# State-space tables computed during the dense projections, kept in DRAM and loaded back; the output stage by token block

## The chip, the cores and the metric

The kernel runs on one core of one Trainium2 chip. The metric is the device time of one execution in microseconds (us). The engines are TensorE (PE: matmuls, with PEld for its weight loads), VectorE (DVE), ScalarE (ACT), GpSimd (POOL) and SyncE (SP, which issues transfers). DMA transfers are issued from SP, ACT and POOL.

## What is computed

One inference step of one decoder layer for a prompt of 1024 tokens and 8 samples of 4 tokens, all in f32 (each large product as three products of a high and a low part):

```python
xn = rms_norm(x, ln1_g); proj = xn @ w_in             # 1024 -> u | q | k | v, 512 each
# S5 group, 32 groups of 64 complex states, 16 channels each
dt = exp(ssm_log_dt); lb = exp(a * dt)                # complex a, lb
bb = ((lb - 1) / a)[..., None] * b
h_t = lb * h_{t-1} + bb @ u_t                         # the scan over tokens
y = Re(c @ h) + d * u;  g = gelu(y)
ssm_out = g * sigmoid(g @ ssm_glu_w)
# differential attention, 4 heads (two softmax maps, ALiBi); samples read paged keys and values
o = rms_norm(attend(q, k, v, lam), subln_g) * (1 - lam0)
x = x + concat(ssm_out, o) @ w_out
x = x + cross_attention(x, 256 memory tokens) @ ca_wo
x = x + (silu(conv3(xn @ ffn_wg)) * (xn @ ffn_wv)) @ ffn_wd
```

The prompt's scan is not run token by token: tokens go in chunks of 8, and tables made of powers of `lb` with `b` and `c` turn each chunk into matmuls. They depend on parameters alone.

## The kernel before

**Stages.** Tokens lie in columns (1056 of them, in blocks TB of 384, 384 and 288; the last block ends with the 32 sample columns). Up to the output projection the work is a set of Python generators that `drive` (L1483) interleaves by weight; the order in which they yield sets the priority of the instructions, and a scheduler then fixes one order for each engine's queue. The streams are: `dense_all` (heads 0 and 1, `dense_u` for the state-space input, heads 2 and 3; on the chip it ends at about 334 us), `params` (parameters of the state space, `ssm_params`), `attention_all` (four heads one after the other), `ssm_tables`, `ssm_datas` and `ssm_outs` (four sets q of 8 groups), `memory_kv` (keys and values of the memory), `samples` (paged attention of the samples) and `sample_state`.

**Tables.** `ssm_setup(q)` (L932) makes the tables of set q: `CLr`, `CLi` (six products of 128x576 on POOL), M in the space of `T` (six of 128x512, on POOL except for q = 3, on DVE), a 128x128 block `Kt` by 16 matmuls `kp` (L963) that goes to DRAM (`k_d`), `ST` by eight transposes `sp` (L976), and `Rr`, `Ri` (six products on POOL). Then POOL clears `T` (L989), and eight transfers on SP write shifted copies of `k_d` into it (L991). `ssm_tables` (L1077) starts after the dense projections ("right" marks the room that they leave), set 1 after attention of head 2, set 2 after the attention ("left") and set 3 after `ssm_data(0)`. The tables use three rooms `sqs[q % 3]` and two `sqs[q % 2]`. `ssm_data(q)` (matmuls `wp`, products and scans on DVE, giving `Hr`, `Hi`) and `ssm_out(q)` (matmuls `yp` with `T` and `CL`, gelu, transposes into `gT[q]`) use them.

**Attention.** `turn(t)` transposes probabilities into `aT`, which has `AB = 2` buffers (L776), and `value(t)` multiplies them with v after every second t.

**Output stage** (from L1493). x comes back from DRAM (`xT_d`) into `Xh`, `Xl` by four transfers on POOL, issued ahead of everything else of the stage (L1498); their room is partly that of the samples' tiles. `gate(d, b, ks)` multiplies `gT` with the glu weights for output block d and token block b, d in the outer loop. After the gates `turn_samples(1, ...)` turns the last sample heads, POOL writes them into the last columns of `mixT` (L1595), and `load_part` (L1528) loads each head's part of `mixT` for the three blocks and splits it over the place where `gT` was split. Then, for each of eight output blocks d, `load_cols` loads 128 columns of `w_out`, and `update_x` adds the product to x.

Of the kernel before, what the change touches and what calls it, by code (L numbers as in the profile page):

```python
# [20 lines left out]
SEQ = 1024  # L21
# [48 lines left out]
def hymba_step(ctx: ExitStack, tc: tile.TileContext, A: dict, O: dict, upto=99, dbg=None):  # L70
# [54 lines left out]
    k_d = dram.tile([512, 128], F32, name="k_d")  # L125
# [121 lines left out]
    nCi = sg.tile([128, 16, 16], F32, name="nCi")  # L247

# [201 lines left out]
    a2 = pool(p2, "a2", 1)  # L450
    hdB = pool(p2, "hdB", 1)
# [33 lines left out]
    st = Carve([hdB.tile([128, SEQ], F32, tag=t, name="scr") for t in ("qT", "kT", "vt", "s3", "s4")])  # L485
# [290 lines left out]
    AB = 2  # L776
# [92 lines left out]
    def params():  # L869
        yield from ssm_params(st, ps_t)  # L870
        done.add('params')

# [5 lines left out]
    gp = gT = sk = sd = ptb = sa = mk_ = zs = ps_w = ps_y = ps_x = Bbr = Bbi = M16 = fin = None  # L878
# [5 lines left out]
    def blk(pl, src, name, tag=None):  # L884
        b = pl.tile([128, 16, 2, 16], F32, name=name, tag=tag or name)
# [3 lines left out]
        return b  # L889

    def open_right():
        nonlocal sk, ptb, sa, mk_, Bbr, Bbi, M16, fin
        sk = pool(pk, "sk", 1, side="right")
        Bbr, Bbi = blk(sk, Br, "Bbr"), blk(sk, Bi, "Bbi")
        M16 = sk.tile([128, 16], F32, name="M16")
        nc.vector.tensor_reduce(out=M16, in_=ident.rearrange("p (g c) -> p c g", c=16), axis=AX.X, op=ALU.add)
# [32 lines left out]
    RE = 'GGGGGGGGGGVG'  # L929
    eng = {'G': nc.gpsimd, 'V': nc.vector}  # L930

    def ssm_setup(q):  # L932
        P4 = slice(4 * q, 4 * q + 4)
        sq_, st_ = sqs[q % 3], sqs[q % 2]
        tg = 'ta' if q > 1 else 'td'
        e, e2, e3 = (eng[c] for c in RE[3 * q:3 * q + 3])
        q1 = sk.tile([128, 4, 9, 16], F32, tag="q1", name="q1")
        q2 = sk.tile([128, 4, 9, 16], F32, tag="q2", name="q2")
        CLr = sq_.tile([128, 4, 9, 16], F32, tag="CLr", name="CLr")
        CLi = sq_.tile([128, 4, 9, 16], F32, tag="CLi", name="CLi")  # L940
# [13 lines left out]
        T = sq_.tile([128, 8, 128], F32, tag="T", name="T")  # L954
        Mr, Mi = (T[:, 4 * i:4 * i + 4].rearrange("p r (j c) -> p r j c", c=16) for i in range(2))
        cmul(e2, Mr, Mi, Rv[:, 0, P4].unsqueeze(3).to_broadcast(sh), Rv[:, 1, P4].unsqueeze(3).to_broadcast(sh),
# [3 lines left out]
        kp = tp("kp", tg)  # L960
# [5 lines left out]
        Kt = st_.tile([128, 128], F32, tag="Kt", name="Kt")  # L966
        nc.vector.scalar_tensor_tensor(out=Kt[:, 0:16], in0=M16, scalar=GT[:, 120 + q:121 + q], in1=kp[:, 0:16],
                                       op0=ALU.mult, op1=ALU.add)
        nc.scalar.copy(Kt[:, 16:], kp[:, 16:128])
        nc.scalar.dma_start(out=k_d[128 * q:128 * q + 128, :], in_=Kt)  # L970
        yield Z[2]
        ST = []
        for M in (Mr, Mi):
            sp = tp("sp", tg)
            for r in range(4):
                nc.tensor.transpose(sp[:, 128 * r:128 * r + 128], M[:, r].rearrange("p a b -> p (a b)"), ident)  # L976
            s = st_.tile([128, 4, 128], F32, tag=f"ST{len(ST)}", name="ST")
            nc.scalar.copy(fl(s), sp)
            ST.append(s)
            yield 440  # L980
        Rr = st_.tile([128, 4, 128], F32, tag="Rr", name="Rr")
        Ri = st_.tile([128, 4, 128], F32, tag="Ri", name="Ri")
        sh = [128, 4, 8, 16]
# [118 lines left out]
    def ssm_outs():  # L1102
        for q in range(4):
            yield from until(lambda: q in half)
            yield from ssm_out(q)
# [1013 lines left out]
```

## Time and profile before

| | us |
|---|---|
| median of 3 runs (lowest to highest) | 1847.84 (1842.98 to 1848.39) |
| the profiled execution | 1845.88 |
| its span, first to last instruction | 1844.1 |

The rest of the profiled execution's time, 1.8 us, lies around the span. An engine's busy time is not a cost by itself: where one engine is always busy, only its work counts; where none is, the waits between them do. The granted clock is the share of full speed that TensorE was given in a stretch; its two levels are 1.2 and 2.4 GHz.

### The profile page before, as it was taken

How to read it: one execution, taken by the hardware profiler on the slowest of the kernel's cores; microseconds unless marked ns; L12 is line 12 of the kernel's file. 1: busy time of each engine (PE TensorE's matmuls, PEld its weight loads, DVE VectorE, ACT ScalarE, POOL GpSimd, SP SyncE). 2: the span in 40 equal slices, each digit the busy share in tenths (PEclk: the TensorE clock that was granted, in tenths of full speed). 3: DMA queues.
4: the chain of work that ended last, by engine and by line, in shares of the span. 5: the costliest groups of instructions: out<-in, count | busy, mean ns of one | idle time of the engine just before them, and what ended most of it. 6: DMA issues, size and time to landing. Idle time of an engine off the chain costs nothing.

```text
span 1844.1 us, 28603 instructions
## 1 busy us (share of the span) xinstructions
PE 1717.8 (93%) x11121; PEld 1597.5 (87%) x11121; DVE 1105.2 (60%) x2569; ACT 604.1 (33%) x1368; POOL 487.8 (26%) x543
## 2 busy tenths in 40 slices
PE   8798999779787789999989999999999999999998
PEld 7587897558575689999868999999999999999998
DVE  7866446774896465655546664665555654655653
ACT  6554355545354243444533211111111111111112
POOL 4412411470710034100022332312322222223200
PEclk9898999789797989999989999999999999999999
DMA  5601212143365631233363021211101101201102
GB/s 172 233 26 59 64 48 60 59 127 121 117 204 179 239 90 51 87 98 98 98 196 107 24 61 35 58 32 50 58 24 58 58 24 58 58 24 59 55 15 96
DMA packets 151744, 155.76 MB, mean 84 GB/s; under 512 B 12535, under 2 KB 128915, under 8 KB 151610
## 3 DMA queue, kind: packets, MB, share of 16 engines
q1 hardware_dynamic: 131954, 106.57, 19.5%
q0 software_dynamic: 9152, 27.49, 4.6%
q10 hardware_dynamic: 10504, 19.88, 2.9%
q8 instruction: 87, 1.43, 0.3%
q14 instruction: 47, 0.39, 0.1%
HBM read 124.39 MB, written 29.51 MB: 83 GB/s over the span
## 4 chain that ended last, share of the span: by engine, by line
PE 78%; DVE 10%; DMA 4%; ACT 3%; issue 2%; POOL 0%; ACTq 0%; SPq 0%; DVEq 0%; POOLq 0%
PE pp L184 5%; PE pp L185 5%; PE pp L186 5%; PE pd L186 5%; PE pd L185 4%; PE pd L184 4%; PE pv L186 4%; PE pv L184 4%; PE pv L185 4%; PE pg L184 4%; PE pg L185 4%; PE pg L186 4%; PE pj L184 2%; PE pj L186 2%; PE pj L185 2%
## 5 line engine op out<-in xcount | busy, mean ns | idle before, releaser
L56 DVE TENSOR_TENSOR xacc<-xacc,pd 128x384 f32<-128x384 f32 (+1 forms) x264 | 135.1, 518 | 170.1 <-PE pd L186 170.1
L56 ACT CAST whi<-raw 128x1024 fp32r<-128x1024 f32 x74 | 77.6, 1050 | 435.6 <-PE pg L185 331.6
L186 PE MATMUL pv<-Xh,wlo 128*128 128x384 f32 (+1 forms) x528 | 171.8, 326 | 0.3 <-DVE wlo L56 0.3
L184 PE MATMUL pv<-Xh,whi 128*128 128x384 f32 (+1 forms) x528 | 172.1, 326 | 0.0
L185 PE MATMUL pv<-Xl,whi 128*128 128x384 f32 (+1 forms) x528 | 171.8, 325 | 0.0
L184 PE MATMUL pg<-Xh,whi 128*128 128x384 f32 (+1 forms) x528 | 171.3, 324 | 0.4 <-DVE hg L56 0.4
L184 PE MATMUL pd<-ah,dhi 128*128 128x384 f32 (+1 forms) x528 | 171.2, 325 | 0.1
L186 PE MATMUL pd<-ah,dlo 128*128 128x384 f32 (+1 forms) x528 | 170.9, 324 | 0.0
L185 PE MATMUL pd<-al,dhi 128*128 128x384 f32 (+1 forms) x528 | 170.1, 322 | 0.5 <-DVE al L56 0.5
L185 PE MATMUL pg<-Xl,whi 128*128 128x384 f32 (+1 forms) x528 | 170.6, 323 | 0.0
L186 PE MATMUL pg<-Xh,wlo 128*128 128x384 f32 (+1 forms) x528 | 170.1, 322 | 0.0
L184 PE MATMUL pp<-Mh,whi 128*128 128x384 f32 (+1 forms) x336 | 108.6, 332 | 18.5 <-ACT Mh L56 18.5
L56 DVE TENSOR_TENSOR wlo<-raw,whi 128x1024 fp32r<-128x1024 f32 x74 | 107.1, 1450 | 25.3 <-ACT whi L56 21.9
L793 POOL TENSOR_TENSOR raw<-raw,GT 128x1024 f32<-128x1024 f32 x30 | 70.6, 2354 | 163.4 <-DMA raw<-in_ffn_wg_dram 112.9
L185 PE MATMUL pp<-Ml,whi 128*128 128x384 f32 (+1 forms) x336 | 110.1, 330 | 0.2 <-DVE Ml L56 0.2
L186 PE MATMUL pp<-Mh,wlo 128*128 128x384 f32 (+1 forms) x336 | 110.0, 329 | 0.0
L184 PE MATMUL pj<-whi,Xh 128*128 128x384 f32 (+1 forms) x288 | 101.3, 353 | 5.6 <-DVE vt L56 4.0
L186 PEld LDWEIGHTS pv<-Xh,wlo 128*128 128x128 f32 x528 | 100.1, 190 | 0.5 <-DVE wlo L56 0.4
L186 PE MATMUL pj<-whi,Xl 128*128 128x384 f32 (+1 forms) x288 | 100.4, 349 | 0.0
L184 PEld LDWEIGHTS pv<-Xh,whi 128*128 128x128 f32 x528 | 100.1, 190 | 0.0
L185 PEld LDWEIGHTS pv<-Xl,whi 128*128 128x128 f32 x528 | 100.0, 189 | 0.0
L185 PEld LDWEIGHTS pd<-al,dhi 128*128 128x128 f32 x528 | 99.2, 188 | 0.8 <-DVE al L56 0.8
(792 smaller groups left out, 4514.5 us busy)
## 6 DMA issues: line engine op xcount, KB each, us to landing
raw<-in_ffn_wg_dram SPq DMA_DIRECT2D x22, 512.0 KB, 3.8
raw<-in_ffn_wv_dram SPq DMA_DIRECT2D x22, 512.0 KB, 3.8
raw<-in_ffn_wd_dram SPq DMA_DIRECT2D x22, 512.0 KB, 3.8
pg<-in_cache_k_dram SPq DMA_DIRECT2D x32, 256.0 KB, 2.7
V<-in_cache_v_dram SPq DMA_DIRECT2D x32, 256.0 KB, 5.2
kt<-in_cache_mem_k_dram SPq DMA_DIRECT2D x32, 256.0 KB, 2.8
vt<-in_cache_mem_v_dram POOLq DMA_DIRECT2D x16, 512.0 KB, 5.5
raw<-in_w_in_dram SPq DMA_DIRECT2D x48, 128.0 KB, 3.1
```

The source lines that it names most:

```text
L56: return f(*a, **k)
L184: nc.tensor.matmul(out, lhsT=wh, rhs=xh, start=start, stop=False)
L185: nc.tensor.matmul(out, lhsT=wh, rhs=xl, start=False, stop=False)
L186: nc.tensor.matmul(out, lhsT=wl, rhs=xh, start=False, stop=stop)
L793: nc.gpsimd.tensor_tensor(out=raw, in0=raw, in1=g.unsqueeze(2).to_broadcast([128, KD, 128]), op=ALU.mult)
```

## The change

- `params` goes on after the parameters with all four `ssm_setup(q)`, so that they run beside the dense projections. All their products are on POOL. They work in a pool `tb` of their own, and each set is written to DRAM: `cl_d` and `rr_d` from POOL, `st_d` and `k_d` from ACT. `Kt` is 240 columns wide, with 112 columns of zeros ahead, so that `T` needs no clearing.
- `ssm_load(q)`, called where `ssm_setup(q)` was, brings set q back by eleven transfers on POOL's queue. The conditions of sets 2 and 3 are new.
- `Bbr`, `Bbi` and `M16` are made early and live in a permanent pool. To make room the attention buffer `aT` is single (`AB = 1`) and one scratch tile is gone.
- In the output stage the gates run by token block, the sample heads are turned after block 1, the parts of block b are loaded after its gates, and x is loaded for each output block d on SP, ahead of that block's weights.

```diff
@@ tables
-    k_d = dram.tile([512, 128], F32, name="k_d")
+    k_d = dram.tile([512, 240], F32, name="k_d")
+    cl_d = dram.tile([4, 128, 1152], F32, name="cl_d")
+    st_d = dram.tile([4, 128, 1024], F32, name="st_d")
+    rr_d = dram.tile([4, 128, 1024], F32, name="rr_d")
...
+    tb = pool(p2, "tb", 1)
...
-    AB = 2
+    AB = 1
...
     def params():
         yield from ssm_params(st, ps_t)
+        blk(Bbr, Br)
+        blk(Bbi, Bi)
+        nc.vector.tensor_reduce(out=M16, in_=ident.rearrange("p (g c) -> p c g", c=16), axis=AX.X, op=ALU.add)
         done.add('params')
+        for q in range(4):
+            yield from ssm_setup(q)
...
     def ssm_setup(q):
-        tg = 'ta' if q > 1 else 'td'
-        e, e2, e3 = (eng[c] for c in RE[3 * q:3 * q + 3])
+        e = nc.gpsimd
+        CL = tb.tile([128, 2, 4, 9, 16], F32, tag="CL", name="CLt")
...
+        nc.gpsimd.dma_start(out=cl_d[q], in_=CL.rearrange("p i r j c -> p (i r j c)"))
...
-        kp = tp("kp", tg)
+        kp = tp("kp", "td")
...
-        Kt = st_.tile([128, 128], F32, tag="Kt", name="Kt")
+        Kt = tb.tile([128, 240], F32, tag="Kt", name="Kt")
+        nc.gpsimd.memset(Kt[:, 0:112], 0.0)
...
+        nc.scalar.dma_start(out=st_d[q], in_=ST.rearrange("p i n -> p (i n)"))
...
-        nc.gpsimd.memset(T, 0.0)
+        nc.gpsimd.dma_start(out=rr_d[q], in_=R_.rearrange("p i r n -> p (i r n)"))
+        yield 10
+
+    def ssm_load(q):
+        sq_, st_ = sqs[q % 3], sqs[q % 2]
+        ST = st_.tile([128, 2, 4, 128], F32, tag="ST", name="ST")
+        R_ = st_.tile([128, 2, 4, 128], F32, tag="R", name="Rr")
+        CL = sq_.tile([128, 2, 4, 9, 16], F32, tag="CL", name="CL")
+        T = sq_.tile([128, 8, 128], F32, tag="T", name="T")
+        nc.gpsimd.dma_start(out=ST.rearrange("p i r n -> p (i r n)"), in_=st_d[q])
+        nc.gpsimd.dma_start(out=R_.rearrange("p i r n -> p (i r n)"), in_=rr_d[q])
         for j in range(8):
-            nc.sync.dma_start(out=T[16 * j:16 * j + 16, :, 16 * j:],
-                              in_=k_d[128 * q:128 * q + 128, :128 - 16 * j].rearrange("(g c) f -> c g f", c=16))
+            nc.gpsimd.dma_start(out=T[16 * j:16 * j + 16],
+                                in_=k_d[128 * q:128 * q + 128, 112 - 16 * j:240 - 16 * j]
+                                .rearrange("(g c) f -> c g f", c=16))
+        nc.gpsimd.dma_start(out=CL.rearrange("p i r j c -> p (i r j c)"), in_=cl_d[q])
...
     def ssm_tables():
         yield from until(lambda: 'right' in done)
-        yield from ssm_setup(0)
+        ssm_load(0)
         yield from until(lambda: 2 in done)
         phA.close()
         sqs.append(pool(pk, "sqB", 1, side="right"))
-        yield from ssm_setup(1)
-        yield from until(lambda: 'left' in done)
-        yield from ssm_setup(2)
-        yield from until(lambda: ('data', D3) in done)
-        yield from ssm_setup(3)
+        ssm_load(1)
+        yield from until(lambda: 'left' in done and ('data', 0) in done)
+        ssm_load(2)
+        yield from until(lambda: ('data', 1) in done and ('out', 0) in done)
+        ssm_load(3)
@@ output stage
-    for k in range(0, KD, 4):
-        for i, X in enumerate((Xh, Xl)):
-            nc.gpsimd.dma_start(out=r32(X[:, k:k + 4]),
-                                in_=xT_d[i][128 * k:128 * k + 512, :].rearrange("(k p) n -> p k n", p=128))
...
-        for d in range(4):
-            for b in range(3):
+        for b in range(3):
+            for d in range(4):
                 if (d, b) not in early:
                     gate(d, b, (0, 1, 2, 3))
-        turn_samples(1, tail['os'], ps.tile([128, 512], F32, tag="pj", name="po"))
-        nc.gpsimd.dma_start(out=mixT[:, SEQ:].rearrange("(h p) t -> p h t", p=128), in_=qsT)
-        for h in range(NH):
-            load_part(wx, Mh, Ml, mixT, 128 * h, 4 + h)
+            if b == 1:
+                turn_samples(1, tail['os'], ps.tile([128, 512], F32, tag="pj", name="po"))
+                nc.gpsimd.dma_start(out=mixT[:, SEQ:].rearrange("(h p) t -> p h t", p=128), in_=qsT)
+            for h in range(NH):
+                load_part(wx, Mh, Ml, mixT, 128 * h, 4 + h, b)
         for d in range(KD):
+            for i, X in enumerate((Xh, Xl)):
+                nc.sync.dma_start(out=r32(X[:, d]), in_=xT_d[i][128 * d:128 * d + 128, :])
             hi, lo = load_cols(A['w_out'][0], d)
```

## Rows read from the trace of the kernel before

**Rows 1.** the page: the span, and the busy time of each engine.

```profile
span 1844.1 us, 28603 instructions
PE 1717.8 (93%) x11121; PEld 1597.5 (87%) x11121; DVE 1105.2 (60%) x2569; ACT 604.1 (33%) x1368; POOL 487.8 (26%) x543
```

**Rows 2.** busy PE, PEld, DVE, ACT, POOL by stretch; PEclk, DMA, GB/s.

```profile
95.00:334.00 239.00, 230.96 (x1322) 197.48 (x1321) 130.04 (x441) 118.35 (x389) 54.48 (x78) 0.97 0.17 49
334.00:446.00 112.00, 85.76 (x649) 67.89 (x647) 81.29 (x224) 59.19 (x150) 56.71 (x55) 0.82 0.37 111
...
466.00:560.00 94.00, 78.79 (x742) 64.60 (x742) 81.24 (x149) 38.27 (x69) 41.35 (x36) 0.85 0.57 173
560.00:590.00 30.00, 18.13 (x158) 12.46 (x154) 28.18 (x74) 17.05 (x31) 0.00 (x0) 0.72 0.43 125
...
620.60:634.50 13.90, 13.90 (x86) 13.62 (x84) 4.68 (x9) 3.02 (x6) 3.49 (x5) 1.00 0.97 347
634.50:650.60 16.10, 0.03 (x1) 0.00 (x0) 0.01 (x1) 0.43 (x1) 0.00 (x0) 0.60 0.83 316
650.60:660.00 9.40, 9.39 (x46) 9.39 (x47) 6.06 (x12) 4.28 (x9) 0.00 (x0) 0.77 0.49 141
```

**Rows 3.** the chain of waits, 466 to 650 us: start, us, what.

```profile
623.33 24.58 DMA mixT<-qsT
```

**Rows 4.** timeline of POOL: start, us, instruction [idle before it, releaser].

```profile
620.34 0.79 POOL L1498 DMA_DIRECT2D Xh<-xT_h  x1 [84.69 <-DMA ms<-mixT]
...
623.33 0.76 POOL L1595 DMA_DIRECT2D mixT<-qsT  x1
```

**Rows 5.** what PE waited for, 334 to 620 us: total, times, longest.

```profile
PE yp L1052 <- DVE Hr L56: 11.2, 3, 7.4
...
PE sp L976 <- ACT Kt L56: 4.3, 1, 4.3
```

**Rows 6.** groups on DVE, 334 to 600 us: xcount, busy us, mean ns.

```profile
L56 DVE TENSOR_TENSOR mwl<-mraw,mwh 128x1024 fp32r<-128x1024 f32 x16 | 23.2, 1454 | 17.2 <-ACT mwh L56 17.1
L56 DVE TENSOR_TENSOR_SCAN vr<-rho,vr 128x128 f32<-128x128 f32 x16 | 9.4, 643 | 0.0
...
L56 DVE TENSOR_TENSOR vr<-va,vb 128x512 f32<-128x512 f32 x4 | 7.1, 1775 | 0.0
L56 DVE TENSOR_TENSOR_SCAN vi<-rho,vi 128x128 f32<-128x128 f32 x16 | 6.7, 478 | 0.0
...
L56 DVE TENSOR_SCALAR yk<-vk 128x2 int32<-128x2 int32 x4 | 4.7, 1172 | 0.1
```

**Rows 7.** timeline of DVE at moments when POOL computes nothing.

```profile
446.53 0.17 DVE L56 TENSOR_SCALAR yk<-vk 128x2 int32<-128x2 int32 x1
...
514.93 0.68 DVE L56 TENSOR_TENSOR q<-Rv,Bi 128x512 f32<-128x512 f32 x1
...
538.50 0.67 DVE L56 TENSOR_TENSOR vr<-va,vb 128x512 f32<-128x512 f32 x1
...
540.41 1.36 DVE L56 TENSOR_TENSOR_SCAN vr<-rho,vr 128x128 f32<-128x128 f32 x4
...
542.27 1.22 DVE L56 TENSOR_TENSOR mwl<-mraw,mwh 128x1024 fp32r<-128x1024 f32 x1
```

**Rows 8.** PE and PEld busy, L963 (kp), then L976 (sp), 334 to 620.6 us.

```profile
334.00:620.60 286.60, 3.70 (x64) 2.18 (x64) 0.84 0.45 136
334.00:620.60 286.60, 6.37 (x32) 4.40 (x32) 0.84 0.45 136
```

**Rows 9.** groups on POOL, 334 to 560 us, the costliest.

```profile
L951 POOL TENSOR_TENSOR CLi<-q,q 128x576 f32<-128x576 f32 x4 | 6.5, 1631 | 0.3
```

**Rows 10.** timeline of PE in attention of head 3.

```profile
423.05 1.56 PE L727 MATMUL ov<-aT,vt 128*128 128x256 f32 x6
...
425.54 0.60 PE L719 MATMUL pt<-ident,P 128*128 128x128 f32 x4
```

**Rows 11.** transfers: issuer, xcount, KB each, median us to landing.

```profile
Ug<-u_p SPq DMA_DIRECT2D x4, 512.0 KB, 4.4
```

More of the change, by code (lines that the diff above doesn't have):

```diff
@@ L247, in hymba_step @@
     nCi = sg.tile([128, 16, 16], F32, name="nCi")
+    Bbr, Bbi = (sg.tile([128, 16, 2, 16], F32, name=n) for n in ("Bbr", "Bbi"))
+    M16 = sg.tile([128, 16], F32, name="M16")
     px = ctx.enter_context(ExitStack())
@@ L484, in hymba_step @@
     xt_ = [load_x(0)]
-    st = Carve([hdB.tile([128, SEQ], F32, tag=t, name="scr") for t in ("qT", "kT", "vt", "s3", "s4")])
+    st = Carve([hdB.tile([128, SEQ], F32, tag=t, name="scr") for t in ("qT", "kT", "vt", "s3")])
     grow = st.tile([128, 128], F32, name="grow")
@@ L882, in tp, with blk @@
         return ps_t.tile([128, 512], F32, tag=tag, name=name)
-    def blk(pl, src, name, tag=None):
-        b = pl.tile([128, 16, 2, 16], F32, name=name, tag=tag or name)
+    def blk(b, src):
         nc.gpsimd.memset(b, 0.0)
@@ L888, in blk @@
         nc.scalar.copy(b[64:128, :, 1, :], src[64:128])
-        return b
     def open_right():
-        nonlocal sk, ptb, sa, mk_, Bbr, Bbi, M16, fin
+        nonlocal sk, ptb, sa, mk_, fin
         sk = pool(pk, "sk", 1, side="right")
-        Bbr, Bbi = blk(sk, Br, "Bbr"), blk(sk, Bi, "Bbi")
-        M16 = sk.tile([128, 16], F32, name="M16")
-        nc.vector.tensor_reduce(out=M16, in_=ident.rearrange("p (g c) -> p c g", c=16), axis=AX.X, op=ALU.add)
         fin = sk.tile([128, 2, 16], F32, name="fin")
@@ L951, in ssm_setup @@
         e.tensor_tensor(out=CLi, in0=q1, in1=q2, op=ALU.subtract)
+        nc.gpsimd.dma_start(out=cl_d[q], in_=CL.rearrange("p i r j c -> p (i r j c)"))
         yield Z[0]
         sh = [128, 4, 8, 16]
[L954 to L956 removed]
+        M = tb.tile([128, 2, 4, 128], F32, tag="M", name="M")
+        cmul(e, M[:, 0].rearrange("p r (j c) -> p r j c", c=16), M[:, 1].rearrange("p r (j c) -> p r j c", c=16),
+             Rv[:, 0, P4].unsqueeze(3).to_broadcast(sh), Rv[:, 1, P4].unsqueeze(3).to_broadcast(sh),
              Br[:, P4].unsqueeze(2).to_broadcast(sh), Bi[:, P4].unsqueeze(2).to_broadcast(sh),
@@ L970, in ssm_setup @@
         nc.scalar.dma_start(out=k_d[128 * q:128 * q + 128, :], in_=Kt)
         yield Z[2]
-        ST = []
-        for M in (Mr, Mi):
-            sp = tp("sp", tg)
+        ST = tb.tile([128, 2, 512], F32, tag="ST", name="STt")
+        for i in range(2):
+            sp = tp("sp", "td")
             for r in range(4):
[L976 to L979, printed above, removed]
+                nc.tensor.transpose(sp[:, 128 * r:128 * r + 128], M[:, i, r], ident)
+            nc.scalar.copy(ST[:, i], sp)
@@ L1105, in ssm_outs @@
             yield from ssm_out(q)
+            done.add(('out', q))
     def ssm_sample(s):
@@ L1138, in ssm_sample @@
         hs = bus
-        Cbr, Cbi = blk(s, Cr, "Cbr", "uz"), blk(s, nCi, "Cbi", "bT")
+        Cbr, Cbi = (s.tile([128, 16, 2, 16], F32, name="Cb", tag=t) for t in ("uz", "bT"))
+        blk(Cbr, Cr)
+        blk(Cbi, nCi)
         st1 = s.tile([128, 16, 8], F32, name="st1")
@@ L1526, in token_rstd, with load_part @@
         rsqrt(pl, r, v, 9)
-    def load_part(pl, Mh, Ml, src, row, k):
-        for t0, n in TB:
-            ms = pl.tile([128, 384], F32, tag="xn", name="ms", bufs=4)
-            nc.sync.dma_start(out=ms[:, :n], in_=src[row:row + 128, t0:t0 + n])
-            split(Mh[k][:, t0:t0 + n], Ml[k][:, t0:t0 + n], ms[:, :n])
+    def load_part(pl, Mh, Ml, src, row, k, b):
+        t0, n = TB[b]
+        ms = pl.tile([128, 384], F32, tag="xn", name="ms", bufs=4)
+        nc.sync.dma_start(out=ms[:, :n], in_=src[row:row + 128, t0:t0 + n])
+        split(Mh[k][:, t0:t0 + n], Ml[k][:, t0:t0 + n], ms[:, :n])
     def load_cols_k(w, d):
```

25 lines of the change are left out of this document (9 added, 16 removed).

## The prediction, made before the changed kernel was run

> **What bounds the kernel now.** I read the busy shares first: TensorE (PE) is busy 93% of 1844.1 us [rows 1]. So a change pays only where PE idles or runs at the lower clock, and the next view is the table of stretches [rows 2]. It shows three kinds of stage. In the dense projections, 95 to 334 us, PE is busy 231.0 of 239.0 us: PE is the bound, 8.0 us are idle, and GpSimd (POOL) works only 54.5 us. From 334 to 590 us the last attention head, the memory keys, the samples and the state space run together, and no engine is full for long: PE is busy 85.8 of 112.0, then 78.8 of 94.0, then 18.1 of 30.0 us, at granted clocks of 0.82, 0.85 and 0.72. VectorE (DVE) is the busiest one there from 466 us on, with 81.2 of 94.0 and 28.2 of 30.0 us; these two stretches are near DVE's bound. In the third kind, at the output projection, PE does nothing for 16.1 us (634.5 to 650.6) and then starts at a granted clock of 0.77.
>
> The chain of waits says whose that last hole is: a single write, the 32 sample columns of the heads (mixT<-qsT), takes 24.58 us to land [rows 3]. POOL's timeline shows why: it was issued at 623.33, right behind the loads of x (4 issues of 2112 KB, from 620.34) on the same queue [rows 4]. The loads of the head parts, in order on SP, wait for that write from the third one on, and PE, at 0.03 us of matmuls in 16.10 us, waits for those [rows 2].
>
> **Part 1, the output stage.** Three edits act together. The gates run block by block, so the part loads of blocks 0 and 1 no longer stand behind the sample columns. The sample write no longer has the x loads ahead of it. And x comes in 16 loads of 528 KB on SP, behind the parts. PE then has matmuls of blocks 0 and 1 for output blocks d = 0, 1, ... while the sample columns travel; six accumulators of 24 matmuls at 0.16 us (86 in the 13.90 us before the hole [rows 2]) cover about 23 us. The hole goes: 16.1 us. So does the restart: 9.4 us at 0.77 of the clock means 4.3 us at the lower of the two levels, which cost half of that, 2.2 us [rows 2]. Sum: 18.3 us saved. The lower bound is 8: the sample output may now be wanted by PE earlier than it is ready, since only the gates of the last block stand between, or the first weights may queue on SP behind an x load that waits for its room until the samples end (before, at 620.34 [rows 4]). The upper bound is 20.
>
> By the Trainium skill, page "DMA: Bandwidth & Descriptors", section "Issuing engines are not separate DMA queues", transfers issued by different engines run on the same 16 DMA engines, and another issuer saves only issue time. By that, moving x from POOL to SP is worth nothing in itself, and what counts is that x is asked for after the parts and in small pieces. If it still overtook them, this part would be worth nothing, which is rival 4.
>
> **Part 2, the tables leave the stage from 334 to 590 us.** Each of four sets is 18 POOL products in this stage, except that one product set of q = 3 ran on DVE; a product lasts about 1.3 to 1.6 us (the longest group 1631 ns) [rows 9], and POOL is busy 56.7 and 41.4 us here [rows 2], most of it this. POOL itself is off the path. Its price is seen on DVE: the four scans take 1.36 us, one 128x512 addition 0.67 us, one weight remainder (mwl) 1.22 us and one tiny yk 0.17 us while POOL computes nothing [rows 7], but their means over the stage are 643 and 478 ns a scan, 1775, 1454 and 1172 ns [rows 6]. The excess of these five groups: 16 x (0.643 - 0.340) = 4.8, 16 x (0.478 - 0.340) = 2.2, 4 x (1.775 - 0.67) = 4.4, 16 x (1.454 - 1.22) = 3.7 and 4 x (1.172 - 0.17) = 4.0, together 19.1 us. To it come six products of q = 3 on DVE at 0.68, 4.1 us [rows 7], and one direct wait of PE for a table (sp<-Kt), 4.3 us [rows 5]. Total 27.5 us. How much is on the path? In 466 to 590 DVE is full enough that I count all; mwl and yk lie largely in 334 to 446, where DVE is busy 81.3 of 112.0, and count half. That leaves some 24 us. Bounds: 5 (only the direct wait, the rest filled by other waits such as PE for Hr, 11.2 us [rows 5], which stay because the order data, out, data, out stays) and 45 (nearly all idle time of PE in the three stretches, 26.2 + 15.2 + 11.9 = 53.3 us, goes with them).
>
> **Part 3, where they go.** Into the dense projections, behind the parameters, spread by the driver's weights over about 95 to 334 us. PE gets 64 small matmuls and 32 transposes there, 3.70 + 6.37 = 10.1 us at the mixed clock of the old place [rows 8], say 8 at the clock of 0.97 here; PE is the bound here, so all 8 count. POOL rises from 54 to about 160 of 239 us: not full, and its other work (scaling of weights, output of u) has double buffers behind it. DVE, 130 of 239 us, takes over the excess above, but with room. PE's waits here were 8.0 us in all; I add 6. The accumulator tag td gains 12 uses, included. Sum 14 us lost; bounds 6 and 35.
>
> **Part 4, the trip through DRAM.** Per set three writes and eleven loads. The nearest load, a 512 KB Ug, lands in 4.4 us [rows 11]; the loads are asked for a head or a data step ahead, so I cost them at nothing on the path. What hides them is attention of head 3 for sets 0 and 1, and data 1 and out 1 for sets 2 and 3. Without that cover a set costs one landing plus eleven issues of about 0.76 us [rows 4] on POOL, some 13 us. POOL's loads of sets 2 and 3 wait for old buffers (data 0, out 0), and the sample state's rows and its memsets stand behind them on POOL; SP loses its T loads, which helps the page loads. Bounds 0 and +8.
>
> **Part 5, free edits.** One attention buffer instead of two (AB): PE's timeline has the next pair's transposes only after the value matmuls of the pair before (423.05 to 425.54) [rows 10], so the one buffer is read out before it is wanted: nothing, at worst the 1.5 us of such a row a few times. One scratch tile fewer and larger permanent tables: room only, nothing; at worst an added wait of a few us.
>
> **Sum.** 1845.9 us of the profiled run (span 1844.1 and 1.8 around it; median of the runs 1847.8) - 18.3 - 24 + 14 + 0 = 1817.6. I forecast 1817 us, its own range 1802 to 1832.
>
> **Rivals.** (1) The contention only moves. The rows on DVE show that POOL's products slow it wherever they meet; in the dense stage DVE's attention work would be late and PE, which runs in its order, would wait. If all 24 us reappear as PE waits: 1842. For it: the DVE rows; against: DVE is at 54% there against 88% in 466 to 590. By the Trainium skill, "GPSIMD Engine Reference", section "Engine selection", elementwise work belongs on VectorE, and its "Key points" say that GpSimd shares SBUF interfaces with it: that speaks against handing the last DVE product to POOL and keeping all of them there. The trace agrees on the contention (1775 against 670 ns). (2) DVE is the bound from 446 us on, and the stage shrinks by the upper bound of 45: 1845.9 - 18.3 - 45 + 14 = 1797. For it: 94% DVE at 560 to 590 and clocks that rise as PE's gaps close. (3) Slower: PE's order. In the dense stage each set puts table matmuls (kp, then sp) into PE's queue, behind six POOL products each; all dense matmuls queue behind a kp that waits. Eight such waits of a whole chain, 6 x 1.63 = 9.8 us, cost 78 us: 1845.9 - 18.3 - 24 + 8 + 78 = 1890. It decides from about 4.3 us a wait on, where the 34 us net gain is eaten. Against: the same pairs cost PE only 4.3 us directly in the old place [rows 5]. (4) The output stage does not do what it says, because x or the sample columns still hold PE: 1845.9 - 24 + 14 = 1836.
>
> **How the numbers follow.** Forecast 0.56, rival 1 0.12, rival 2 0.18, rival 3 0.06, rival 4 0.08. Rival 2 carries the low end to 1788, rivals 4 and 1 the high end to 1842; rival 3 is left out. About 0.3% (5.5 us) is what a measurement here can tell from no change. Rival 1 falls half inside it: faster 0.56 + 0.18 + 0.08 + 0.06 = 0.88, same 0.06, slower 0.06.
>
> **What would show it.** Part 1: no PE wait over a few us between the gates and the output projection, and the sample write landing in under 5 us. Part 2: scans near 340 ns and vr near 670 ns after the dense stage, POOL without products there, the gates starting some 10 to 20 us earlier relative to the dense end. Part 3: dense end 14 us later, at about 348 us. The prediction is wrong if PE's waits for kp, sp or the table loads add up to more than 15 us, or if the stage from the dense end to the gates is as long as before.

## The result and the profile after

The changed kernel takes 1819.2 us (median of 4 runs, 1816.4 to 1823.9) against 1846.2 us of the kernel before on the same chip (4 runs, 1843.0 to 1848.4): a ratio of 0.987, 95% interval 0.984 to 0.989, faster by 27 us. The forecast was 1817 us, inside its own range. The profiled runs, which the views below show, stand at 1845.9 and 1823.9 us, 22 us apart. How close the sum came is luck in part: Part 1 was too large, Part 2 too small, and Part 3 met its size for another reason than the one given. That is what the rest tells.

The head of the page of the kernel after, to be set beside [rows 1]:

```profile
span 1822.0 us, 28691 instructions
PE 1713.6 (94%) x11121; PEld 1596.7 (88%) x11121; DVE 1088.7 (60%) x2563; ACT 602.8 (33%) x1368; POOL 509.3 (28%) x597
```

PE does the same work in a shorter span. Where the time went is read best from three marks on PE: the first matmul of the state space (wp; attention has just ended), the first gate (zp) and the first norm of the next block (pq). They are single rows of PE's timeline (start us, us, instruction), first of the kernel before:

```profile
446.72 1.96 PE L1008 MATMUL wp<-Ug,ST 128*64 128x128 f32 x30
...
590.55 0.69 PE L184 MATMUL zp<-Mh,whi 128*128 128x384 f32 x1
...
749.15 0.65 PE L1688 MATMUL pq<-ones,csq 128*128 128x1 f32 x6
```

and of the kernel after:

```profile
461.96 1.09 PE L1021 MATMUL wp<-Ug,ST 128*64 128x128 f32 x12
...
574.92 0.42 PE L187 MATMUL zp<-Mh,whi 128*128 128x384 f32 x1
...
724.30 0.65 PE L1703 MATMUL pq<-ones,csq 128*128 128x1 f32 x6
```

Their differences cut the span into four stages. The same marks in every kernel of this study, worked out in the same way (us; the last column is the span less the start of pq):

```
kernel           to wp   wp to zp   zp to pq   after pq     span
before           446.7     143.8      158.6     1094.9    1844.1
after            462.0     113.0      149.4     1097.7    1822.0
e1_tail_only     445.7     141.6      147.5     1093.8    1828.6
e2_tables_only   464.1     111.7      161.1     1094.1    1831.1
e3_after_light   438.0     110.9      149.5     1095.6    1794.0
e4_before_light  438.5     133.1      157.4     1098.0    1827.0
e5_after_late    470.1     118.5      148.0     1097.0    1833.6
e6_x_only        450.1     142.8      154.0     1097.8    1844.7
e7_blocks_only   445.3     142.2      152.8     1092.9    1833.1
e8_after_po2     461.1     111.6      153.1     1094.9    1820.8
e9_after_dve     439.6     125.3      147.7     1095.0    1807.7
e10_before_dve   442.1     132.3      136.0     1092.1    1802.4
e11_dve_tail     440.4     131.7      147.4     1093.5    1813.1
e12_late_dve     471.8     124.1      148.4     1097.3    1841.7
```

From before to after: 15.2 us lost up to wp, 30.9 gained in the state stage, 9.2 gained at the output, 2.8 lost in what isn't touched. The last column wanders by 6 us between kernels that are alike there; that is the grain of the table. Every edit also shifts the order of the instructions on all engines, since that order is worked out for the whole program; a few us of a stage can be order alone.

**The state stage.** Groups on VectorE of the kernel after, 80 to 590 us (instructions, then busy us, mean ns of one):

```profile
L56 DVE TENSOR_TENSOR mwl<-mraw,mwh 128x1024 fp32r<-128x1024 f32 x16 | 19.6, 1223 | 6.5 <-ACT mwh L56 6.4
...
L56 DVE TENSOR_TENSOR_SCAN vi<-rho,vi 128x128 f32<-128x128 f32 x16 | 5.5, 405 | 0.1
L56 DVE TENSOR_TENSOR_SCAN vr<-rho,vr 128x128 f32<-128x128 f32 x16 | 5.5, 404 | 0.0
L56 DVE TENSOR_TENSOR vr<-va,vb 128x512 f32<-128x512 f32 x4 | 2.7, 686 | 0.0
L56 DVE TENSOR_SCALAR yk<-vk 128x2 int32<-128x2 int32 x4 | 0.7, 163 | 0.1
```

Against [rows 6]: 1454 ns are 1223, the scans 643 and 478 are 404 and 405, 1775 are 686, 1172 are 163. The waits of PE from 462 to 574.9 us (what waited and for what; total us, times, longest) show what took the place of the old ones:

```profile
PE tp__6483 L1087 <- DVE yt L56: 7.1, 1, 7.1
PE pt L1398 <- DMA pg<-in_cache_k_dram: 7.0, 2, 6.3
...
PE yp L1065 <- DVE Hr L56: 1.3, 1, 1.3
```

The 11.2 us for Hr of [rows 5] are 1.3, and the 4.3 us for the table are gone. New are a wait of 7.1 us for yt, the last step of a set's output on VectorE, and one of 7.0 us for a page of cached keys. Where most of the second sits is seen in the stretch from 480 to 500 us (busy PE, PEld, DVE, ACT, POOL; PEclk, share of the DMA engines, GB/s):

```profile
480.00:500.00 20.00, 13.01 (x112) 11.33 (x111) 11.06 (x37) 6.98 (x15) 9.47 (x18) 0.68 1.03 248
```

The transfers of 470 to 510 us name the company that the pages keep (issues, KB each, median us to landing):

```profile
pg<-in_cache_k_dram SPq DMA_DIRECT2D x10, 256.0 KB, 3.3
...
T<-k_d POOLq DMA_DIRECT2D x16, 64.0 KB, 7.8
```

Two table sets are loaded back there (eight loads of T for each), and the DMA engines are full from 480 to 500 us.

**The dense stage.** The last projection matmul ends at 372.3 us and not at 334.9 (attention had come further by then, so the mark at wp is the fairer one). From 80 to 120 us, first before, then after:

```profile
80.00:120.00 40.00, 36.90 (x199) 31.48 (x199) 32.10 (x102) 22.62 (x79) 18.71 (x30) 0.96 0.22 63
```

```profile
80.00:120.00 40.00, 24.64 (x109) 16.74 (x107) 28.47 (x65) 13.82 (x39) 32.25 (x46) 0.75 0.23 71
```

POOL works 13.5 us more and PE 12.3 us less, at a lower clock. What hangs between them is seen on VectorE's smallest instructions, two groups of 80 to 320 us (durations in ns: least, median, longest), first before, then after:

```profile
L56 DVE TENSOR_TENSOR rs_t<-rsq x30: 147/166/1874, 81.5 to 319.5; 128x8 f32<-128x8 f32 x24, 32x4 f32<-32x4 f32 x6
L56 DVE SCALAR_TENSOR_TENSOR cc<-cc,nlam,ssum x20: 210/220/272, 84.7 to 314.5; 128x1 f32<-128x1 f32 x20
```

```profile
L56 DVE TENSOR_TENSOR rs_t<-rsq x23: 142/167/5085, 84.3 to 318.1; 128x8 f32<-128x8 f32 x18, 32x4 f32<-32x4 f32 x5
L56 DVE SCALAR_TENSOR_TENSOR cc<-cc,nlam,ssum x16: 207/220/3378, 92.4 to 303.6; 128x1 f32<-128x1 f32 x16
```

By their means the 128x8 form of the first takes 583 ns for 170 and the second 678 for 222. But the medians are the same: most of these instructions are not slowed at all, and a few are held. Of VectorE's operations on 8, 4 or 1 numbers a row between 80 and 320 us, 15 last longer than 0.5 us in the kernel after (6 in the kernel before), and each of the 15 ends within 0.05 us after an instruction of POOL has ended. The longest hold, followed on VectorE, POOL and PE (start us, us, instruction):

```profile
84.27 5.08 DVE L56 TENSOR_TENSOR rs_t<-rsq 128x8 f32<-128x8 f32 x1
```

```profile
88.17 1.15 POOL L953 TENSOR_TENSOR q<-Cr,Li 128x576 f32<-128x576 f32 x1
```

```profile
92.57 0.61 DVE L56 SCALAR_TENSOR_TENSOR wlo<-raw,G,whi 128x384 fp32r<-128x384 f32 x1
```

```profile
93.24 0.69 PE L188 MATMUL pj<-wlo,Xh 128*128 128x384 f32 x1 [5.95 <-DVE wlo L56]
```

The small step is held until the table product has ended (89.32). A split of weights that stands behind it in VectorE's order comes late, and PE waits 5.95 us for that split, which takes no operand from the held step. PE's waits for VectorE from 80 to 320 us add up to 7.9 us before and 23.2 after, 15.3 more; the loss up to wp is 15.2. The largest row of each, first before, then after (three more of the latter, for P, mx and vt, have 3.9 to 5.0 us):

```profile
PE bc L767 <- DVE y L56: 4.0, 1, 4.0
```

```profile
PE pj L188 <- DVE wlo L56: 6.3, 2, 5.9
```

**The output stage.** PE's waits from 573 to 655 us, and the landings of the transfers on mixT (write and part loads together):

```profile
PE po L1356 <- DVE os__5850 L56: 5.4, 1, 5.4
```

```profile
DMA to landing us min/median/max: 2.3/2.5/6.0
```

The wait of 16.1 us before the output matmuls [rows 2] is gone, and the write of 24.58 us [rows 3] takes 6.0; PE now waits 5.4 us for the sample output, which it meets earlier than VectorE has it.

### The profile page after: what moved, and what is told of

Its sections match the earlier page's. It is cut to its first block, busy times and chain, and to the rows that moved or that the text cites. A ratio compares the mean times of both kernels' runs of the same rounds, so it can differ in the third digit from the quotient of the medians.

```text
span 1822.0 us, 28691 instructions
## 1 busy us (share of the span) xinstructions
PE 1713.6 (94%) x11121; PEld 1596.7 (88%) x11121; DVE 1088.7 (60%) x2563; ACT 602.8 (33%) x1368; POOL 509.3 (28%) x597
## 4 chain that ended last, share of the span: by engine, by line
PE 79%; DVE 8%; ACT 4%; DMA 3%; issue 1%; SPq 1%; ACTq 0%; POOL 0%; DVEq 0%; POOLq 0%
PE pp L187 5%; PE pp L188 5%; PE pp L189 5%; PE pv L189 5%; PE pv L187 5%; PE pv L188 5%; PE pd L189 5%; PE pd L188 5%; PE pd L187 5%; PE pg L187 5%; PE pg L188 5%; PE pg L189 4%; PE pj L187 2%; PE S L694 2%; PE pj L189 2%; PE pj L188 2%
## 5 line engine op out<-in xcount | busy, mean ns | idle before, releaser
L188 PE MATMUL pj<-wlo,Xh 128*128 128x384 f32 (+1 forms) x288 | 100.5, 350 | 6.3 <-DVE wlo L56 6.3
```

Of the source, the lines that this page charges most:

```text
L188: nc.tensor.matmul(out, lhsT=wh, rhs=xl, start=False, stop=False)
```

## Experiments

Ratios are to the kernel before on the same chip, with 95% intervals; differences in us are between medians. The theory on trial is that of the prediction: the tables' products on POOL slow VectorE, moving them frees the state stage, the dense stage pays 14 us for PE work and waits, and the output stage loses its hole.

### One half at a time: e1_tail_only and e2_tables_only

e1 is the kernel before with the output stage of the kernel after; e2 is the kernel after with the output stage of before. A part of e1's edit (x and the parts change as in the diff of the change):

```diff
-        for d in range(4):
-            for b in range(3):
+        for b in range(3):
+            for d in range(4):
                 if (d, b) not in early:
                     gate(d, b, (0, 1, 2, 3))
```

> The kernel before with the changed output stage alone (gates and head parts by token block, sample output behind block 1, x loaded per output block); tables stay where they were. My theory: the hole behind the sample write closes, 18 us off in the range 8 to 20, so a ratio to before of 0.990 (0.989 to 0.996), 1826 to 1838 us; no PE wait over 6 us between the last gate and the first output block, the sample write landing in under 5 us. Rival (the wait for the sample output, queued ahead of the gates of block 2, and the x loads give it back): ratio 0.997 to 1.000, with a PE wait of 10 us or more on po or on X.

> The changed tables alone (computed in the dense stage, stored, loaded back); the output stage is the one of before. My theory: parts 2 and 3 together give 24 - 14 = 10 us, ratio 0.9946, 1836 us, and the 16 us hole behind the sample write is still there. If the two parts add up to what the whole change gave (27 us), this one and the tail alone sum to 27. Rival (contention only moves): ratio 0.999 to 1.002, 1843 to 1849. Rival (DVE bound, the state stage shrinks by 45): ratio 0.984 or less, 1816 or less. In the profile: dense end at about 372 us, first gate at about 575, as in the kernel after.

e1: 1831.5 us, 0.992 (0.990 to 0.994), 14 us off. e2: 1830.6 us, 0.991 (0.989 to 0.993), 15 us off. Together 29.8, the whole change 26.9: the halves add up within their error. The output stage is worth less than the 18 of the sum, the tables more than its 10; by the stages, e2 pays 17.4 us up to wp and gains 32.1 from wp to zp. Rivals 1 and 4 in their pure form are out, and so is rival 2 for the total.

### What the products cost in either place: e3_after_light and e4_before_light

```diff
-        e.tensor_tensor(out=q1, in0=cr, in1=lr, op=ALU.mult)
-        e.tensor_tensor(out=q2, in0=ci, in1=li, op=ALU.mult)
-        e.tensor_tensor(out=CLr, in0=q1, in1=q2, op=ALU.add)
+        e.tensor_tensor(out=CLr, in0=cr, in1=lr, op=ALU.mult)
...
```

> The kernel after with a third of the tables' products: each table is written by one product instead of two products and a sum (24 instead of 72 POOL instructions; the tables hold other numbers, so what is computed from them is left out of the reference's sense). PE, DVE, ACT and DMA have the same work. Theory A (the dense stage grew by 37 us because the POOL products slow VectorE, whose excess beside POOL is some 46 us between 80 and 320): two thirds of it goes, dense end back to some 350 us, and the time falls by 12 to 25 us, ratio to before 0.973 to 0.980. Theory B (the growth is the 8 us of PE work, the order and the waits of the table steps): dense end stays within 5 us of 372, ratio to before 0.984 to 0.988, like the kernel after.

> The kernel before with the same cut: a third of the tables' products, each table written by one product (what is computed from the tables is left out of the reference's sense). They run between 334 and 590 us here. My theory: the products' price in that stage is DVE slowed beside POOL, 19.1 us of excess, 4.1 us of products on DVE and 4.3 us of PE's wait; two thirds of it goes, 13 to 18 us, ratio 0.990 to 0.993. Rival (DVE's slowness there is not from these products, or is hidden): under 5 us, ratio 0.997 to 1.000. Rival (the products hold the stage by more than I counted): 30 us or more, ratio under 0.984.

e3: 1796.4 us, 0.973 (0.971 to 0.975), 23 us below the kernel after. e4: 1823.8 us, 0.988 (0.986 to 0.989), 22 us below the kernel before. Two thirds of the products cost the same in the dense stage as in the old place. (e4's own theory had said 13 to 18 us, its rival 30 or more: neither was met.) So the 15 us of e2 aren't slowness that has vanished: it moved, at its full price. And the dense stage's loss is of this kind. With PE's table work still in it and only products taken out, e3 reaches wp at 438.0 us, like e4 (438.5), which has three sets of that work after wp; PE's waits for VectorE from 80 to 320 us are back at 8.1 us. Theory A of e3 holds; what the sum charged there (8 us of PE work, 6 us of waits) isn't to be seen. Between the same two kernels the stage from wp to zp is 22.2 us shorter in e3: that is what the move gives apart from most of the slowness. PE's waits there for the state space fell (in the full kernels Hr 11.2, vb 5.5, Kt 4.3 us before; 1.3, none, none after), while the two new ones above, 14.1 us, came in; what makes up the 22.2 no run took one by one.

### When the sets start: e5_after_late

```diff
         done.add('params')
+        yield from until(lambda: ('head', 1) in done)
         for q in range(4):
             yield from ssm_setup(q)
+            done.add(('set', q))
...
     def ssm_tables():
         yield from until(lambda: 'right' in done)
+        yield from until(lambda: ('set', 3) in done)
         ssm_load(0)
```

> The kernel after with one change: the table sets start only once head 1's projections have begun, and not in the middle of the parameters (the first table products stand at 79 us in the kernel after, ahead of the last steps of the parameters, and PE is busy 25 of the 40 us from 80 to 120 where it was 37 of 40 before). Theory A (what the dense stage lost is above all this place, where VectorE already works 39 of 40 us): 12 us or more come back, ratio to before 0.976 to 0.981. Theory B (the products cost the same wherever they stand beside VectorE's work, as the 23 us of the cut in the kernel after and the 22 us of the same cut in the kernel before suggest): within 4 us of the kernel after, ratio 0.985 to 0.989.

1835.7 us, 0.996 (0.994 to 0.997): 16 us slower than the kernel after, where theory A expected 12 faster and B no change. Both fell. wp comes 8.2 us later, the stage behind it is 5.5 us longer. The edit has a second half: the first load waits until all four sets are made. PE has no wait for a table load ahead of wp here or in e12. (From 80 to 120 us VectorE was busy 28.5 of 40 us in the kernel after, as shown above, and not 39.) e12 takes this up.

### Which edit closes the hole: e6_x_only and e7_blocks_only

e6 changes only the x loads of the kernel before, e7 only the order of gates and parts. The edit of e6:

```diff
-            nc.gpsimd.dma_start(out=r32(X[:, k:k + 4]),
-                                in_=xT_d[i][128 * k:128 * k + 512, :].rearrange("(k p) n -> p k n", p=128))
...
         for d in range(KD):
+            for i, X in enumerate((Xh, Xl)):
+                nc.sync.dma_start(out=r32(X[:, d]), in_=xT_d[i][128 * d:128 * d + 128, :])
```

> The kernel before with only its x loads changed: two loads for each output block on SP's queue in place of four big ones on POOL ahead of the sample write. Gates and parts stay in the order of before. Theory A (the hole is the sample write waiting for the big loads that were issued just before it): the wait of pp for Mh, 16.1 us, falls to 3 to 6 us (write, load and split of the last part), ratio 0.992 to 0.995. Theory B (the hole is the order: no output matmul can start until all parts have come back): the wait stays above 10 us, ratio 0.997 or more.

> The kernel before with only the order changed: gates and head parts by token block, the sample output behind block 1; x still comes in four big loads on POOL ahead of the sample write. Theory A (big loads ahead of the write): the write still lands 20 us or more after its issue, but only block 2 waits for it, and the first two blocks give 8 us of matmuls ahead of it: 4 to 9 us off, ratio 0.995 to 0.998. Theory B (the order is what counts): all of the 14 us of the tail alone, ratio 0.992.

e6: 1841.5 us, 0.999 (0.998 to 1.001). e7: 1835.0 us, 0.997 (0.996 to 0.999), some 5 us by the ratio. Neither makes the 14 us of e1, and by the ratios they make 6 together. From zp to pq of the profiled runs they gain 4.6 and 5.8 us, which is nearly e1's 11.1, so these numbers don't say that the edits are worth more together than apart. PE's waits, 570 to 680 us, of e6 and then of e7, and the landings on mixT in e7:

```profile
PE pp L184 <- ACT Mh L56: 10.8, 2, 10.4
```

```profile
PE po L1340 <- DVE os__5787 L56: 5.8, 1, 5.8
PE pp L184 <- ACT Mh L56: 3.4, 1, 3.4
```

```profile
DMA to landing us min/median/max: 2.2/2.5/25.1
```

In e7 the write still takes 25.1 us to land behind the big loads, and only block 2 waits for it, as theory A had it. In e6 the write lands in 6.5 us, yet 10.4 us of the hole stay. That is theory B's sign, but SP's timeline of e6 shows a third cause:

```profile
623.49 0.90 SPq L1527 DMA_DIRECT2D ms<-mixT  x2
...
635.68 4.16 SPq L1596 DMA_DIRECT2D Xh<-xT_h  x1
639.95 1.91 SPq L1527 DMA_DIRECT2D ms<-mixT  x4
```

Between the second part load and the third stand eleven x loads, so the third is asked for some 9 us after the write has landed (issued at 624.32). x overtook the parts, as in rival 4. So e6 doesn't test the order alone, and the prediction's own step, x behind the parts, isn't in it. e10 below keeps the old order, its write lands in 7.1 us and its parts have no x load ahead of them on SP: PE waits for no part. By that the hole of the kernel before comes from the late write; the order by blocks hides a part of it. The rule weighed in Part 1 (the Trainium skill, "DMA: Bandwidth & Descriptors", "Issuing engines are not separate DMA queues": another issuing engine saves issue time alone) would give e6's time, 0.999, but e6 is no test of it, since its x loads are also smaller and stand in another order.

### The sample output later: e8_after_po2

```diff
-            if b == 1:
+            if b == 2:
                 turn_samples(1, tail['os'], ps.tile([128, 512], F32, tag="pj", name="po"))
```

> The kernel after with the sample output turned behind the gates of block 2 instead of block 1. PE waits 5.4 us for os ahead of that turn in the kernel after, because VectorE has not yet reached it. If that wait is simply time lost, it goes: 4 to 5 us, ratio to before 0.983 to 0.985. If the write, load and split of block 2's parts then come late (landing 2.3 to 6 us each), PE waits as long ahead of the third output block: within 2 us of the kernel after, ratio 0.986 to 0.988.

1821.9 us, 0.988 (0.987 to 0.990), no different from the kernel after. The wait changes its name, in PE's waits of 570 to 680 us:

```profile
PE pp L187 <- ACT Mh L56: 9.1, 1, 9.1
```

5.4 us for os became 9.1 us for the last parts. The sample columns come late; meeting them one block later gained nothing.

### Products on VectorE: e9_after_dve and e10_before_dve

```diff
-        e = nc.gpsimd
+        e = nc.vector
```

in the kernel after; in the kernel before the string of engines:

```diff
-    RE = 'GGGGGGGGGGVG'
+    RE = 'VVVVVVVVVVVV'
```

> The kernel after with all 72 table products on VectorE instead of POOL. Theory A (the price of the products is what they do to VectorE's own instructions while both run: between 80 and 320 us a 128x8 operation takes 583 ns where it took 170 in the kernel before, a 128x1 one 678 for 222, the 128x384 split 833 for 702; on VectorE a product of 128x512 takes about 0.69 us, so 72 of them add 51 us of work to an engine that is busy 141 of these 240 us, but nothing is slowed): a gain of 5 to 15 us on the kernel after, ratio to before 0.979 to 0.984. Theory B (VectorE's time is what counts, whoever takes it: 51 us of work in place of some 31 us of slowness): a loss of 5 to 20 us on the kernel after, ratio 0.989 to 0.998.

> The kernel before with all 72 table products on VectorE (6 of them are there already). They run between 334 and 590 us, where VectorE is the busiest engine but PE. Theory A (slowness beside POOL goes, scans back from 643 and 478 ns to about 405, the one 128x512 sum from 1775 to about 690): 66 products by 0.69 us add 46 us to VectorE and take off up to 54 us of its slowness, 0 to 10 us faster, ratio 0.994 to 1.000. Theory B (VectorE's time counts and its queue stands in order, so that what PE waits for, Hr and vb, comes behind the products): 10 to 30 us slower, ratio 1.005 to 1.016.

e9: 1809.3 us, 0.981 (0.979 to 0.984), 10 us below the kernel after. e10: 1806.3 us, 0.979 (0.976 to 0.982), 39 us below the kernel before. Theory A holds in e9; in e10 its sign holds, by far more than the 10 us that it had allowed. Groups of e10 on VectorE, 80 to 590 us:

```profile
L56 DVE TENSOR_TENSOR_SCAN vr<-rho,vr 128x128 f32<-128x128 f32 x16 | 5.4, 403 | 0.0
```

The slowness is gone though VectorE does 66 more products. Each product is also quicker there (means of 0.68 to 0.90 us for 1.06 to 1.74), and e10 doesn't part the two. By the stages 16.2 us come ahead of zp. Another 22.6 lie between zp and pq, where nothing was edited: the samples' last matmuls start at 573.8 us instead of 607.4, so POOL's timeline now has 18 us between the last x load and the sample write, where [rows 4] has the write right behind the loads, and PE waits for no part:

```profile
583.16 0.75 POOL L1498 DMA_DIRECT2D Xl<-xT_l  x1
601.33 0.76 POOL L1595 DMA_DIRECT2D mixT<-qsT  x1 [17.42 <-DVE qsT L56]
```

So one changed string beats the whole change by 13 us. Up to zp it gains what the move gains (16.2 us against 15.6 in the kernel after); that it closes the hole as well is luck of the order, and e11 shows how easily it is lost. The Trainium skill, "GPSIMD Engine Reference", section "Engine selection", puts elementwise work on VectorE; both runs agree, by 10 us and by the 16.2 us ahead of zp.

### Products on VectorE with the changed output stage: e11_dve_tail

e10 with the output stage of e1.

> The kernel before with the table products on VectorE and the changed output stage; the tables stay in the stage where they were. If the two are separate prices, 39 + 14 = 53 us off, ratio to before 0.971, 1792 us. If the products on VectorE had closed the output stage's hole already (there the x loads were issued 20 us ahead of the sample write and PE waited for no part), the output stage adds nothing: within 4 us of the products alone, ratio 0.977 to 0.981, 1802 to 1810 us. Set against the kernel after with its products on VectorE (1809 us), which has the same output stage, it also prices the place of the tables alone: if moving them is worth something without the slowness, this one is slower than 1809.

1817.0 us, 0.987 (0.985 to 0.989): neither sum nor no change, but 11 us slower than e10. Up to zp it is 2 us ahead of e10; between zp and pq it loses 11.4. PE's waits from 583 to 630 us have one row:

```profile
PE zp L184 <- ACT th L56: 9.6, 1, 9.6
```

A gate waits for the tanh of an earlier gate. ScalarE's timeline says what that stood behind, and SP's timeline why (both of e11; of the 16 x loads the first and the last, then the part loads):

```profile
603.38 1.54 ACT L56 CAST Mh<-ms 128x384 fp32r<-128x384 f32 x3 [8.28 <-DMA ms<-mixT]
604.83 0.49 ACT L56 ACTIVATE th<-zp 128x384 f32<-128x384 f32 x1
```

```profile
578.17 0.33 SPq L1597 DMA_DIRECT2D Xh<-xT_h  x1
...
592.06 0.32 SPq L1597 DMA_DIRECT2D Xl<-xT_l  x1
593.46 4.43 SPq L1527 DMA_DIRECT2D ms<-mixT  x4
```

The part loads stand behind 14 us of x loads on SP, ScalarE's split of the parts waits for them, the tanh behind it too, and PE with it. In the kernel after the same 16 loads come behind the first 8 part loads. This is the place that the lower bound of Part 1 and rival 4 named (x overtaking); there it didn't happen, here and in e6 it did.

Against e9, which has the same output stage and the same engine for the products, zp comes at 572.1 and not 565.0 us: with the products on VectorE the place of the tables is worth 7 us up to there.

### Late sets on VectorE: e12_late_dve

e5, with both halves of its edit, and `e = nc.vector`.

> The late table sets of the second experiment on the kernel after (they start once head 1's projections have begun; 16 us slower than the kernel after), now with their products on VectorE. Theory A (late sets cost more because they slow VectorE where it has more to do, 13.9 us between 280 and 320): without POOL the late start costs nothing, 1805 to 1814 us, ratio 0.979 to 0.984. Theory B (the late start itself, the order of PE's queue and the later attention, costs the 16 us): 1820 us or more, ratio 0.987 or more.

1843.4 us, 0.998 (0.997 to 1.000), 34 us slower than e9. Theory B: the late start costs by itself, 32 of it up to wp. VectorE's timeline (start us, us, instruction) shows the products in the middle of the normalisation of head 0, whose links are rs_t and y:

```profile
180.61 0.17 DVE L56 TENSOR_SCALAR y<-v 128x8 int32<-128x8 int32 x1
...
180.81 0.74 DVE L56 TENSOR_TENSOR CLt<-q,q 128x576 f32<-128x576 f32 x1
181.47 0.16 DVE L56 TENSOR_TENSOR rs_t<-y 128x8 f32<-128x8 f32 x1
...
183.01 0.16 DVE L56 TENSOR_TENSOR rs_t<-rs_t,v 128x8 f32<-128x8 f32 x1
```

The links of 0.16 us start 0.9 and 1.5 us after the one before, and products stand in order between them. At the end of the chain stand head 0's last matmuls (bc<-y), which the next stage waits for. PE's waits, 155 to 205 us, name kp, which stands in PE's queue behind the same engine:

```profile
PE kp L969 <- DVE rs_t L56: 5.8, 1, 5.8
PE bc L773 <- DVE y L56: 2.1, 1, 2.1
```

These two are 8 of the 32 us. Over the whole stretch up to wp, first e12, then e9:

```profile
0.00:471.80 471.80, 404.04 (x2455) 338.48 (x2455) 302.92 (x1105) 237.58 (x726) 129.11 (x223) 0.90 0.37 115
```

```profile
0.00:439.60 439.60, 391.86 (x2451) 325.91 (x2451) 306.12 (x1112) 240.93 (x728) 130.51 (x224) 0.95 0.40 125
```

PE is idle 67.8 us against 47.7, and busy 12.2 us longer with the same matmuls, at a granted clock of 0.90 against 0.95. So 20 us are idle time and 12 the lower clock; which product held which wait, beyond the two rows above, wasn't traced.

## Why the prediction was right, and where it was not

**The forecast.** 1817 predicted, 1819 measured; the sum's change of 28.3 us against 27. Part 1's surplus (4 us by medians, 7 by stages) and Part 2's deficit (7) cancelled, and Part 3 met its size by a mechanism that the sum had ruled out; that the total fits is luck to that extent. The low end of 1788 is worked out from no row. The cases lie as follows.

**Part 1 (18.3).** Right in mechanism, too large: 14.4 us by medians in e1, 11.1 by its stages. The hole of 16.1 us went. The mis-sized step is the one that gave its lower bound: PE meets the sample output before VectorE has it, 5.4 us in the kernel after and 5.7 in e1. That the three edits act together, as Part 1 had it, is not shown: e6 and e7 gain nearly as much apart as e1 does by the stages, and e6 has x ahead of the parts. e6 and e11 show rival 4 happening once the order of SP's queue turns. Nothing in the change holds that order.

**Part 2 (24 on the path).** The stage gained 30.9 to 32.1 us (kernel after, e2), within the bounds, above the 24. By the groups of the kernel after the excess of the five is 16 x (0.643 - 0.404) + 16 x (0.478 - 0.405) + 4 x (1.775 - 0.686) + 16 x (1.454 - 1.223) + 4 x (1.172 - 0.163) = 17.1 us where the sum had 19.1: the 1.36 us of [rows 7] are four scans that overlap, and one alone takes at least 398 ns in the same trace. And two of the terms count one moment of the kernel before twice:

```profile
466.43 4.18 DVE L56 TENSOR_SCALAR yk<-vk 128x2 int32<-128x2 int32 x1
...
466.52 4.09 DVE L56 TENSOR_TENSOR vr<-va,vb 128x512 f32<-128x512 f32 x1
```

Both end at 470.61, with a product on POOL (469.42 and 1.16 us). That is all of yk's excess and 3.4 of the 4.4 us of vr's; it lies at 466 and not in 334 to 446, where the sum had halved yk. The step that was too small is the one that counted PE's wait for Hr as staying: it fell from 11.2 to 1.3 us.

**Part 3 (14).** The size was near (15.2 and 17.4 us up to wp), the make-up wrong. The step that failed is "DVE takes over the excess above, but with room". Busy shares said that VectorE was 54% busy and could absorb it. What the runs show instead: single instructions are held until POOL's instruction ends, what stands behind them in VectorE's order comes late, and PE's waits for VectorE grow from 7.9 to 23.2 us. With a third of the products (e3) wp comes at 438.0 us, and with all of them on VectorE (e9) at 439.6, so the loss is the products' being on POOL. PE's table work, 9.4 us by the rows of kp (4.53) and sp (4.91), cost nothing that shows: e3, with all of it ahead of wp, gets there no later than e4. The waits of kp that rival 3 priced were 1.4 us in all, for Bbi. (The longest group of products in the old place is not the 1631 ns of [rows 9] but T<-q,q with 1739; nothing but rival 3's price hangs on it.) The 14 us came from the wrong term.

**Rival 1** was right about the price and wrong about the time. The contention did move, and cost as much as before (e3, e4); but the move also took PE's waits out of the state stage. The two errors, in Part 2 and in what Part 3 is made of, are one: slowness beside POOL was taken for the price of a crowded stage, while cutting the products gains 22 to 23 us in either place.

**Part 4 (0).** Too low within its bounds: table loads fill the DMA engines from 480 to 500 us and PE waits 7.0 us for a page of keys (4.8 in e2, 7.2 in e3), none of which the kernel before has there. The sum had expected the page loads to gain. **Part 5** left nothing that can be told apart from Part 3.

**The marks that the text had set.** No PE wait over a few us at the output: 5.4. Sample write under 5 us: 6.0. Scans near 340: 404. vr near 670: 686. Dense end at 348: 372. Gates 10 to 20 us earlier relative to the dense end: 53 earlier, because attention was further on by then; a mark on attention's end would have told more. Waits for kp and the like under 15 us: yes.

**What stays open.** What the move is worth with no slowness at all, 7 us (e9 against e11) or 23 (e3 against e4, up to zp); why these differ wasn't taken apart. Why late sets cost 24 us more than the two traced waits. How much of e10's gain is quicker products and how much the holds that went. Whether the parts of the output stage are worth more together. And an e10 whose sample order is fixed by the program, and not by luck, wasn't run; e10 as it stands has the lowest median of the kernels here that leave nothing out, 3 us below e9, and their intervals overlap.

## What to carry over

Before moving work because it disturbs another engine, put it on that engine once and measure: here that took one string and gave as much up to the first gate as the move with all its tables, 16 us. Don't read an engine's room from its busy share alone, or slowness from a mean: look at the longest instructions of a group, and at what the other engine was doing when they ended. And where two edits are meant to act together, test them alone and together, and check that each test alone hasn't changed the queue that they share.

## What the runs showed of the hardware

- While POOL computes, single instructions of VectorE were held until an instruction of POOL had ended: 15 of the smallest between 80 and 320 us in the kernel after, each ending within 0.05 us of one, the longest held 5.08 us. Medians did not move (166 and 167 ns for rs_t<-rsq, 220 for cc), so a group's mean tells how often it was held and not how slow it is. A hold could outlast one product: the one of 5.08 us spans several instructions of POOL, the 3.38 us of cc too.
- In the kernel after the custom operation P<-S on 128x512 was not held in that stretch (685 ns, 684 before), nor was rsq<-rs_t,rsq on 128x8 (169 ns at most); in e3 the latter has one of 1845 ns, so a group that wasn't held in one run isn't safe in another.
- A product on POOL is also slow itself: the shortest groups of 128x512 products have means of 1058 to 1094 ns on POOL in the kernel after; VectorE takes 0.68 us [rows 7].
- Where PE has holes its granted clock is lower too, between its two levels of 1.2 and 2.4 GHz: 0.75 from 80 to 120 us with PE busy 24.6 of 40, 0.68 from 480 to 500 with 13.0 of 20; the stretch before the output matmuls, with PE always busy, stands at 1.00 [rows 2]. Behind the hole of 16.1 us PE was busy 9.39 of 9.40 us at 0.77 [rows 2], so that hole cost more than its length.
